# Conv-FFN of a hybrid transformer trunk: the tile epilogue in two parts, half a tile behind, and another order in the pool mixer

## The chip, the cores and the metric

The kernel runs on one core of one Trainium2 chip. Its metric is the device time of one execution in microseconds (us). TensorE (PE) does the matmuls, VectorE (DVE) and ScalarE (ACT) the work on their operands and results, SyncE (SP) starts the DMAs that bring weights, and GpSimd (POOL) does next to nothing. An engine works through its instructions in the order in which the program holds them; engines wait for each other by semaphores. Products collect in PSUM, in eight banks of 2 KB for each of 128 partitions.

## The reference

One step of a trunk of four layers on 384 tokens (128 of context, 256 latent) of width 1024, in f32. The token mixer of a layer is a gated MLP (layers 0 and 3), a pooling mixer (layer 1) or windowed attention (layer 2). A convolutional FFN follows in every layer:

```python
def conv_ffn(h, w_in, conv_w, conv_b, w_out):
    a, u = jnp.split(h @ w_in, 2, axis=-1)
    ap = jnp.pad(a, ((0, 0), (1, 1), (0, 0)))
    a = ap[:, :-2] * conv_w[0] + ap[:, 1:-1] * conv_w[1] + ap[:, 2:] * conv_w[2] + conv_b
    return (jax.nn.gelu(a) * u) @ w_out

# run_trunk, for every layer i
h = rms_norm(x, g_mix[i]) * (1 + sc1) + sh1
y = ...                                        # the mixer
x = x + gt1 * y
h = rms_norm(x, g_ffn[i]) * (1 + sc2) + sh2
x = x + gt2 * conv_ffn(h, w_ffn_in[i], ffn_conv_w[i], ffn_conv_b[i], w_ffn_out[i])
```

The shifts, scales and gates (sh, sc, gt) come from `silu(cond) @ w_ada + b_ada`, six vectors a layer ("adaLN" below). The inner width is 2816, so `w_in` gives 22 tiles of 128 columns of `a` and as many of `u`. The pooling mixer subtracts from each token the mean over a window around it (four window sizes, one for each group of 256 columns), and multiplies each group by a 256x256 matrix.

## The kernel before

**Weights.** All weights lie in one list of chunks of 128x1024 f32, in the order of use; SP streams them into five buffers (`wraw`). For more precise products each chunk is split in two: ACT copies it to the rounded `whi` (L353), DVE subtracts that from it to get `wlo` (L360). Activations are split in the same way: in `split_act` ACT makes `gh` or `hb` (L592), DVE `gl` or its twin (L593). `mm3` (L678) then issues three matmuls for each product: `whi` with the high part, `wlo` with the high part, `whi` with the low part. `w_get` takes the next chunk for PE and first issues the split (`w_split`) of the chunk that comes three later; a function given as `mid` is called between the `whi` and the `wlo` of that split. Four buffers hold split chunks.

**adaLN.** Chunks of `w_ada` are woven into the list between the weights of other layers' work. Each costs DVE two instructions (`junk`, L395), which `w_split` issues behind `wlo`. The table `EDGES` says how many weights of a phase pass before the first such chunk and how many follow the last; the phase "fi" is the FFN's first product.

**FFN (`ffn`).** The chunks "fr" compute tiles 0 and 1 together in four PSUM banks. Then tile f = 2 to 21 takes two chunks (kk = 0 and 1), each 24 matmuls, in a pair of banks: `pa` gets the convolution's input, `pu` the gate. Six banks rotate under the name `mm`; tile 3 has the two others (`psa` and `adaT`). Each tile has an epilogue in three steps:

- `epi_a`: only for the first NR[l] = 3, 4, 3, 3 tiles of layers 0 to 3, whose input is not yet normalised: DVE scales `pa` and `pu` into SBUF. These tiles leave their banks there.
- `epi_b`: ACT copies `pa` into the padded row `ab` (L722) and starts the convolution `ct` (L724); DVE adds the two other taps (L726, two instructions).
- `epi_c`: ACT's GELU of `ct` into `gg` (L735), DVE's product with the gate (L736), which reads `pu` from PSUM. Then `split_act`.

In tile f's loop pass, `epi_a` and `epi_b` of tile f - 1 come with chunk kk = 0, `epi_c` ahead of chunk kk = 1's split, and `split_act` behind it. Tile 3's epilogue waits until f = 5, where tiles 3 and 4 go together. `norm(3)` issues three steps of the normalised input with each chunk while f < NR[l].

**Pool (`pool`, layer 1).** For each of four groups: `first` multiplies the group's columns (L1022), `scaled` copies the product to SBUF with ACT, scaled by the norm (`u`, three buffers, and `us2`, whose last part DVE makes at L1036), `second` does the windows' means as matmuls (L1045 to L1049) and DVE adds them to `x` (L1052). After each 128 columns of `x`, `aft` makes operands of the FFN that follows. The order is written out at the end of the function.

The scheduler keeps each engine's instructions in the order in which the functions call them.

Of the kernel before, what the change touches and what calls it, by code (L numbers as in the profile page):

```python
# [62 lines left out]
}  # L63


EDGES = {(0, "gv"): (2, 1), (0, "go"): (5, 0), (3, "gv"): (5, 2), "fi": (8, 2), (3, "go"): (5, 2)}


AP_REST = {"qkv": 1}
# [215 lines left out]
class Prog:  # L285
# [395 lines left out]
    def ffn(self, l, pr, follow, stat_k):  # L681
# [6 lines left out]
        with self.tc.tile_pool(name=f"ffn{l}", bufs=1) as fp:  # L688
# [11 lines left out]
            def epi_a(f, pa, pu):  # L700
                if f >= NR[l]:
                    return f, pa, None, pu, None
                a1 = self.tmp.tile([128, T], F32, tag="sq", name="a1")
                nc.vector.tensor_tensor(out=a1, in0=pa[:, 0:T], in1=rbs, op=ALU.mult)
                be = self.tmp.tile([128, 4], F32, tag="be", name="be")
                nc.scalar.activation(be[:, 0:2], pa[:, T:TE], AF.Copy)
                nc.scalar.activation(be[:, 2:4], pu[:, T:TE], AF.Copy)
                u1 = fp.tile([128, T], F32, tag="u1", name="u1", bufs=2)
                nc.vector.tensor_tensor(out=u1, in0=pu[:, 0:T], in1=rbs, op=ALU.mult)
                return f, a1, be, u1, be[:, 2:4]  # L710

            def epi_b(st):
                f, a1, be, _, _ = st
                cw = [self.par[:, PCOLS["cw"][0] + (3 * l + i) * NF + f:][:, 0:1] for i in range(3)]
                cb = self.par[:, PCOLS["cb"][0] + l * NF + f:][:, 0:1]
                ab = abs_[f % 2]
                for c, (t0, t1) in enumerate(GRPS):
                    p0, p1 = pos[c]
                    if f < NR[l]:
                        nc.scalar.activation(ab[:, p0:p1], a1[:, t0:t1], AF.Identity, bias=be[:, c:c + 1])  # L720
                    else:
                        nc.scalar.activation(ab[:, p0:p1], a1[:, t0:t1], AF.Copy)  # L722
                t = self.tmp.tile([128, T + 1], F32, tag="ct", name="ct")
                nc.scalar.activation(t, ab[:, 1:T + 2], AF.Identity, scale=cw[1], bias=cb)  # L724
                for i in (0, 2):
                    nc.vector.scalar_tensor_tensor(out=t, in0=ab[:, i:i + T + 1], scalar=cw[i], in1=t,  # L726
                                                   op0=ALU.mult, op1=ALU.add)
                return t
# [30 lines left out]
            def norm(n):  # L759
                for _ in range(n):  # L760
                    next(steps, None)
# [14 lines left out]
                    if k > stat_k + 1:  # L776
                        norm(2)

            prev = [(0, b[0], b[1]), (1, b[2], b[3])]
            for f in range(2, NF):  # L780
                w0 = TE if f < NR[l] else T

                pa, pu = (p()[:, :w0] for p in ((self.ps_bank, self.px_bank) if f == 3 else (self.bank, self.bank)))
                now, prev = (prev, []) if f == 5 else (prev[:1], prev[1:])
                for kk in range(2):
                    if kk == 0:
                        sts = []
                        w = self.w_get("fi", mid=lambda: sts.extend([epi_a(*p) for p in now]))
                        ts = [epi_b(st) for st in sts]
                    else:  # L790
                        gs = [epi_c(st, t) for st, t in zip(sts, ts)]
                        w = self.w_get("fi")
                        for st, g in zip(sts, gs):
                            self.split_act(g, gh[st[0]], gl[st[0]])
                    if f < NR[l]:
                        norm(3)
                    for k4 in range(4):
                        k = 4 * kk + k4
                        r = (hh[:, k, :], hl[:, k, :]) if f < NR[l] else (nh[:, k, :], nl[:, k, :])
                        self.mm3([(pa, 256 * k4), (pu, 256 * k4 + 128)], w, r, k == 0, k == 7)  # L800
                prev.append((f, pa, pu))
            assert next(steps, 0) == 0 and len(prev) == 1
            sts = []
            self.w_split(self.n_get + 2, lambda: sts.extend([epi_a(*p) for p in prev]))
            g = epi_c(sts[0], epi_b(sts[0]))
            self.split_act(g, gh[NF - 1], gl[NF - 1])
            self.use(1 - self.cur)
            res, after = follow()
            self.out_proj("fo", gh, gl, NF, l, 5, after, mid=self.sqrt_table, after_chunk=1)
# [180 lines left out]
    def pool(self, l, j, prep, pr):  # L990

        nc = self.nc
        hh, hl = self.hh, self.hl
        with self.tc.tile_pool(name=f"pool{l}", bufs=1) as pp:
            mx = pp.tile([128, 4, 640], F32, tag="mx", name="mx")

            ms = pp.tile([66, 4, T], F32R, tag="ms", name="ms")
            us2 = pp.tile([66, 4, 256], F32R, tag="us2", name="us2")  # L1000
            nc.sync.dma_start(mx, self.a["mix"])
            nc.gpsimd.dma_start(ms, self.a["mixsum"])
            nc.gpsimd.memset(us2.bitcast(F32), 0.0)
            res, aft = prep()
            w = None
            us = {}

            def first(g):
                nonlocal w
                if g % 2 == 0:  # L1010
                    w = self.w_get("p")
                ps = [self.bank() for _ in range(2)]
                for i in range(4):
                    o = ps[i // 2][:, 256 * (i % 2):256 * (i % 2) + 256]
                    t = slice(128 * i, 128 * i + 128)
                    if i == 3:
                        o, t = o[0:2, :], slice(T, TE)
                    for p in range(3):
                        for kk in range(2):
                            k = 2 * g + kk  # L1020
                            c = 512 * (g % 2) + 256 * kk
                            nc.tensor.matmul(o, (hl if p == 2 else hh)[:, k, t], w[p == 1][:, c:c + 256],  # L1022
                                             start=(p == 0 and kk == 0), stop=(p == 2 and kk == 1),
                                             skip_group_check=True)
                us[g] = ps

            def scaled(g):
                ps = us[g]
                u = pp.tile([128, 3, 256], F32, tag="u", name="u", bufs=3)
                for i in range(3):  # L1030
                    nc.scalar.activation(u[:, i, :], ps[i // 2][:, 256 * (i % 2):256 * (i % 2) + 256], AF.Copy,
                                         scale=r[:, i:i + 1])
                sh = ps[1][0:2, 256:512]
                for q in (0, 64):
                    nc.scalar.activation(us2[q:q + 2, g, :], sh, AF.Copy)
                nc.vector.tensor_tensor(out=us2[32:34, g, :], in0=sh, in1=us2[0:2, g, :].bitcast(F32), op=ALU.subtract)  # L1036
                us[g] = u

            def second(g):
                u = us.pop(g)  # L1040
                for n in range(2):
                    d = 2 * g + n
                    ps = self.bank()[:, :T]
                    c = slice(128 * n, 128 * n + 128)
                    nc.tensor.matmul(ps, us2[:, g, c], ms[:, g, :], start=True, stop=False, skip_group_check=True)  # L1045
                    nc.tensor.matmul(ps[:, 0:TC], u[:, 0, c], mx[:, g, 0:128], start=False, stop=False,
                                     skip_group_check=True)
                    for i in range(2):
                        nc.tensor.matmul(ps[:, TC:T], u[:, 1 + i, c], mx[:, g, 128 + 256 * i:384 + 256 * i],  # L1049
                                         start=False, stop=(i == 1), skip_group_check=True)  # L1050
                    for cc, (t0, t1) in enumerate(GRPS):
                        nc.vector.scalar_tensor_tensor(out=self.x[:, d, t0:t1], in0=ps[:, t0:t1],  # L1052
                                                       scalar=self.pgs[:, d, cc:cc + 1], in1=self.x[:, d, t0:t1],
                                                       op0=ALU.mult, op1=ALU.add)
                    aft(d)

            first(0)
            r = self.stats(pr["acc"])
            first(1)
            scaled(0)  # L1060
            first(2)
            scaled(1)
            second(0)
            scaled(2)
            first(3)
            second(1)
            scaled(3)
            second(2)
            second(3)
            return res  # L1070
# [626 lines left out]
```

## Time and profile before

| | us |
|---|---|
| three runs, median (lowest to highest) | 1771.77 (1771.72 to 1775.01) |
| the profiled execution | 1772.34 |
| its span | 1770.6 |
| PE busy | 1748.9 |
| PE weight load busy | 1671.1 |
| DVE busy | 1347.4 |
| ACT busy | 885.5 |
| POOL busy | 3.4 |

The granted clock of PE was 0.999 of full speed over the span. Busy times come from one profiled execution; a merged row of the timeline covers successive instructions of one form, and matmuls overlap, so that a row's time is longer than the pitch between them. A wait is the idle time of an engine ahead of an instruction, put down to the instruction whose semaphore came last.

### The profile page before, as it was taken

The numbers are of one execution on the slowest core, as the hardware profiler recorded it, in microseconds if no ns is written. First come the engines' busy times: TensorE is split into PE (matmuls) and PEld (weight loads), VectorE is DVE, ScalarE is ACT, GpSimd is POOL, SyncE is SP. The second block draws the span as 40 slices with busy tenths as digits, with TensorE's granted clock in tenths as the row PEclk, the third lists the DMA queues.
The fourth block names the chain that finished last, engine by engine and source line by source line (L and its number), as shares of the span: only waits on it lengthen the run. The fifth ranks groups of instructions, "written<-read, shape, count | busy, mean of one in ns | idle before, by whom it ended". The sixth has DMA issues, their size and how long they took to land.

```text
span 1770.6 us, 26877 instructions
## 1 busy us (share of the span) xinstructions
PE 1748.9 (99%) x10282; PEld 1671.1 (94%) x10282; DVE 1347.4 (76%) x2309; ACT 885.5 (50%) x1661; POOL 3.4 (0%) x32
## 2 busy tenths in 40 slices
PE   9999999999999999999999999999999999999999
PEld 7799899999998999999778999999988999999999
DVE  6888778888986788886787788887775676876632
ACT  4644346444456654532568564553354444754521
POOL 0000000000000000000000000000000000000000
PEclk9999999999999999999999999999999999999999
DMA  9765654565662356566443336556645334354341
GB/s 338 281 220 167 230 196 139 195 199 188 232 219 106 108 190 202 185 226 208 175 150 132 119 132 200 191 173 202 196 166 192 119 132 155 118 180 147 133 155 54
DMA packets 87728, 312.03 MB, mean 176 GB/s; under 512 B 10478, under 2 KB 10990, under 8 KB 87344
## 3 DMA queue, kind: packets, MB, share of 16 engines
q1 hardware_dynamic: 87216, 309.91, 51.4%
q8 instruction: 80, 1.31, 0.3%
q0 software_dynamic: 96, 0.41, 0.1%
q14 instruction: 48, 0.39, 0.1%
q10 hardware_dynamic: 288, 0.01, 0.0%
HBM read 308.45 MB, written 1.84 MB: 175 GB/s over the span
## 4 chain that ended last, share of the span: by engine, by line
PE 79%; DVE 12%; ACT 5%; issue 3%; DMA 2%; ACTq 0%; DVEq 0%; SPq 0%
PE mm L678 60%; PE mm L852 6%; DVE wlo L360 4%; DVE junk L395 4%; ACT whi L353 2%; DMA wraw<-wts 2%; DVE ct L726 2%; PE adaT L678 2%; PE S L678 1%; PE psa L678 1%; PE mm L896 1%; PE S L1133 1%; PE adaT L852 1%; PE psa L852 1%; PE O L1353 0%
## 5 line engine op out<-in xcount | busy, mean ns | idle before, releaser
L678 PE MATMUL mm<-hb,whi 128*128 128x384 f32 (+1 forms) x3936 | 859.2, 337 | 0.0
L678 PEld LDWEIGHTS mm<-hb,whi 128*128 128x128 f32 x3936 | 698.2, 188 | 3.6 <-issue 1.2
L360 DVE TENSOR_TENSOR wlo<-wraw,whi 128x1024 fp32r<-128x1024 f32 (+2 forms) x390 | 466.0, 1201 | 211.7 <-ACT whi L353 211.2
L353 ACT ACTIVATE whi<-wraw 128x1024 fp32r<-128x1024 f32 (+2 forms) x390 | 399.6, 1034 | 252.2 <-PE mm L678 156.1
L678 PE MATMUL mm<-hb,wlo 128*128 128x384 f32 (+1 forms) x1968 | 504.5, 337 | 5.0 <-DVE wlo L360 4.9
L678 PEld LDWEIGHTS mm<-hb,wlo 128*128 128x128 f32 x1968 | 355.9, 188 | 7.8 <-DVE wlo L360 7.8
L395 DVE SCALAR_TENSOR_TENSOR junk<-wraw,condb 128x1024 bf16<-128x1024 f32 x288 | 351.9, 1222 | 7.9 <-ACT condb L1615 2.7
L735 ACT ACTIVATE gg<-ct 128x128 f32<-128x128 f32 (+1 forms) x150 | 46.4, 356 | 245.6 <-DVE ct L726 245.6
L678 PE MATMUL mm<-gh,wlo 128*128 128x384 f32 x448 | 123.3, 336 | 0.6 <-DVE wlo L360 0.6
L678 PE MATMUL mm<-gh,whi 128*128 128x384 f32 x448 | 123.3, 336 | 0.0
L678 PE MATMUL mm<-gl,whi 128*128 128x384 f32 x448 | 123.2, 336 | 0.0
L726 DVE SCALAR_TENSOR_TENSOR ct<-ab,par,ct 128x385 f32<-128x385 f32 x176 | 108.6, 619 | 6.2 <-ACT ct L724 2.5
L852 PE MATMUL mm<-whi,hb 128*128 128x512 f32 x320 | 87.2, 397 | 0.0
L613 ACT ACTIVATE hb<-x,A 128x128 fp32r<-128x128 f32 x96 | 42.5, 455 | 86.1 <-DVE x L468 80.4
L678 PEld LDWEIGHTS mm<-gh,wlo 128*128 128x128 f32 x448 | 81.7, 188 | 1.0 <-DVE wlo L360 1.0
L678 PEld LDWEIGHTS mm<-gh,whi 128*128 128x128 f32 x448 | 81.7, 188 | 0.1
L678 PEld LDWEIGHTS mm<-gl,whi 128*128 128x128 f32 x448 | 81.8, 188 | 0.0
L736 DVE TENSOR_TENSOR gg<-mm,gg 128x384 f32<-128x384 f32 x72 | 40.2, 558 | 47.2 <-ACT gg L735 46.5
L852 PEld LDWEIGHTS mm<-whi,hb 128*128 128x128 f32 x320 | 59.4, 187 | 17.2 <-issue 2.5
L724 ACT ACTIVATE ct<-ab,par 128x385 f32<-128x385 f32 x88 | 62.7, 713 | 3.4
L468 DVE SCALAR_TENSOR_TENSOR x<-mm,prm,x 128x128 f32<-128x128 f32 x92 | 33.6, 411 | 27.0 <-PE mm L678 27.0
L852 PE MATMUL mm<-wlo,hb 128*128 128x512 f32 x160 | 47.0, 399 | 0.0
(291 smaller groups left out, 1769.4 us busy)
## 6 DMA issues: line engine op xcount, KB each, us to landing
wraw<-wts SPq DMA_DIRECT2D x562, 512.0 KB, 3.9
wraw<-wts SPq DMA_DIRECT2D x12, 256.0 KB, 2.9
wraw<-wts SPq DMA_DIRECT2D x8, 384.0 KB, 4.3
x<-x SPq DMA_DIRECT2D x4, 384.0 KB, 4.5
mx<-mix SPq DMA_DIRECT2D x1, 1280.0 KB, 8.3
y<-x SPq DMA_DIRECT2D x3, 384.0 KB, 4.8
condb<-condb SPq DMA_DIRECT2D x1, 1024.0 KB, 6.5
ws<-a_w_s SPq DMA_DIRECT2D x2, 512.0 KB, 5.5
```

Of the source, the lines that this page charges most:

```text
L353: nc.scalar.activation(hi[:, :n], t[:, :n], AF.Copy)
L360: nc.vector.tensor_tensor(out=lo[:, :n], in0=t[:, :n], in1=hi[:, :n].bitcast(F32), op=ALU.subtract)
L395: nc.vector.scalar_tensor_tensor(out=self.junk.bitcast(BF16), in0=w, scalar=1.0, in1=self.condb[:, c, :], op0=ALU.mult, op1=ALU.mult, accu ...
L468: nc.vector.scalar_tensor_tensor(out=x[:, d, t0:t1], in0=ps[:, t0:t1], scalar=self.prm[:, l, ty * 8 + d, c:c + 1], in1=x[:, d, t0:t1], op0 ...
L613: nc.scalar.activation(self.hh[:, d, t0:t1], self.x[:, d, t0:t1], AF.Copy, scale=A[:, d, c:c + 1])
L678: nc.tensor.matmul(o, w[:, c:c + nw], r, start=(first and p == 0), stop=(last and p == 2))
L724: nc.scalar.activation(t, ab[:, 1:T + 2], AF.Identity, scale=cw[1], bias=cb)
L726: nc.vector.scalar_tensor_tensor(out=t, in0=ab[:, i:i + T + 1], scalar=cw[i], in1=t, op0=ALU.mult, op1=ALU.add)
L735: nc.scalar.activation(g[:, t0:t1], t[:, t0 + c:t1 + c], GELU)
L736: nc.vector.tensor_tensor(out=g, in0=u, in1=g, op=ALU.mult)
L852: nc.tensor.matmul(ps[n][i], hs, w[p == 1][:, c:c + 512], start=(k == 0 and p == 0), stop=(k == 7 and p == 2))
L896: nc.tensor.matmul(ps[:, 128 * i:128 * i + 128], v[:, i, 128 * c:128 * c + 128], ws[:, c // 2, :], start=True, stop=True)
```

## The change

One function, `epilogue(todo, get)`, now does the work around each chunk's split. It first takes the chunk (so `whi`, `epi_a` in the middle, `wlo` and adaLN's `junk`), then does `epi_c` and `split_act` of the tile that is due, then `epi_b` of the tile in `todo`, which is due at the next chunk. Tiles up to 3 enter at kk = 0, the others at kk = 1, where before all entered at kk = 0; so from tile 4 on `epi_b` comes one chunk later, and `epi_c` at kk = 0 of the tile after. Layer 1's first adaLN chunk in the FFN comes behind its 14th weight instead of its 11th, with as many in all, and while NR[l] > 3 each chunk takes two normings. In the pool `u` gets a fourth buffer, and `first(3)` comes ahead of `second(0)`.

```diff
@@ -63,7 +63,7 @@
 }
 
 
-EDGES = {(0, "gv"): (2, 1), (0, "go"): (5, 0), (3, "gv"): (5, 2), "fi": (8, 2), (3, "go"): (5, 2)}
+EDGES = {(0, "gv"): (2, 1), (0, "go"): (5, 0), (3, "gv"): (5, 2), (1, "fi"): (12, 2), "fi": (8, 2), (3, "go"): (5, 2)}
 
 
 AP_REST = {"qkv": 1}
@@ -776,34 +776,35 @@
                     if k > stat_k + 1:
                         norm(2)
 
-            prev = [(0, b[0], b[1]), (1, b[2], b[3])]
+
+            prev, due = [(0, b[0], b[1]), (1, b[2], b[3])], []
+
+            def epilogue(todo, get):
+
+                sts = []
+                w = get(lambda: sts.extend([epi_a(*p) for p in todo]))
+                for st, t in due:
+                    self.split_act(epi_c(st, t), gh[st[0]], gl[st[0]])
+                due[:] = [(st, epi_b(st)) for st in sts]
+                return w
+
             for f in range(2, NF):
                 w0 = TE if f < NR[l] else T
 
                 pa, pu = (p()[:, :w0] for p in ((self.ps_bank, self.px_bank) if f == 3 else (self.bank, self.bank)))
-                now, prev = (prev, []) if f == 5 else (prev[:1], prev[1:])
                 for kk in range(2):
-                    if kk == 0:
-                        sts = []
-                        w = self.w_get("fi", mid=lambda: sts.extend([epi_a(*p) for p in now]))
-                        ts = [epi_b(st) for st in sts]
-                    else:
-                        gs = [epi_c(st, t) for st, t in zip(sts, ts)]
-                        w = self.w_get("fi")
-                        for st, g in zip(sts, gs):
-                            self.split_act(g, gh[st[0]], gl[st[0]])
+                    todo = [prev.pop(0)] if f < 6 and kk == 0 or f > 4 and kk == 1 else []
+                    w = epilogue(todo, lambda mid: self.w_get("fi", mid=mid))
                     if f < NR[l]:
-                        norm(3)
+                        norm(2 if NR[l] > 3 else 3)
                     for k4 in range(4):
                         k = 4 * kk + k4
                         r = (hh[:, k, :], hl[:, k, :]) if f < NR[l] else (nh[:, k, :], nl[:, k, :])
                         self.mm3([(pa, 256 * k4), (pu, 256 * k4 + 128)], w, r, k == 0, k == 7)
                 prev.append((f, pa, pu))
             assert next(steps, 0) == 0 and len(prev) == 1
-            sts = []
-            self.w_split(self.n_get + 2, lambda: sts.extend([epi_a(*p) for p in prev]))
-            g = epi_c(sts[0], epi_b(sts[0]))
-            self.split_act(g, gh[NF - 1], gl[NF - 1])
+            epilogue(prev, lambda mid: self.w_split(self.n_get + 2, mid))
+            epilogue([], lambda mid: None)
             self.use(1 - self.cur)
             res, after = follow()
             self.out_proj("fo", gh, gl, NF, l, 5, after, mid=self.sqrt_table, after_chunk=1)
@@ -1026,7 +1027,7 @@
 
             def scaled(g):
                 ps = us[g]
-                u = pp.tile([128, 3, 256], F32, tag="u", name="u", bufs=3)
+                u = pp.tile([128, 3, 256], F32, tag="u", name="u", bufs=4)
                 for i in range(3):
                     nc.scalar.activation(u[:, i, :], ps[i // 2][:, 256 * (i % 2):256 * (i % 2) + 256], AF.Copy,
                                          scale=r[:, i:i + 1])
@@ -1060,11 +1061,11 @@
             scaled(0)
             first(2)
             scaled(1)
+            first(3)
+            scaled(2)
             second(0)
-            scaled(2)
-            first(3)
+            scaled(3)
             second(1)
-            scaled(3)
             second(2)
             second(3)
             return res
```

DVE in layer 0's FFN, from the first part of tiles 3 and 4 (two `ct` pairs on `ab_2351` and `ab_2350`) on, before. `adaT` is tile 3's `pu`; the `mm` under `gg` is that of tile 4, then 5:

```order
L726 SCALAR_TENSOR_TENSOR ct<-ab_2351,par,ct 128x385 x2
L726 SCALAR_TENSOR_TENSOR ct<-ab_2350,par,ct 128x385 x2
L736 TENSOR_TENSOR gg<-adaT,gg 128x384
L736 TENSOR_TENSOR gg<-mm,gg 128x384
L360 TENSOR_TENSOR wlo<-wraw,whi 128x1024
L593 TENSOR_TENSOR gl<-gg,gh 128x384 x2
L360 TENSOR_TENSOR wlo<-wraw,whi 128x1024
L395 SCALAR_TENSOR_TENSOR junk,prm<-wraw,condb 128x1024 x2
L726 SCALAR_TENSOR_TENSOR ct<-ab_2351,par,ct 128x385 x2
L736 TENSOR_TENSOR gg<-mm,gg 128x384
```

Both tiles' `ct` and both `gg` stood together, ahead of the next `wlo`. The same place now, from tile 3's `ct` on:

```order
L726 SCALAR_TENSOR_TENSOR ct<-ab_2351,par,ct 128x385 x2
L360 TENSOR_TENSOR wlo<-wraw,whi 128x1024
L736 TENSOR_TENSOR gg<-adaT,gg 128x384
L593 TENSOR_TENSOR gl<-gg,gh 128x384
L726 SCALAR_TENSOR_TENSOR ct<-ab_2350,par,ct 128x385 x2
L360 TENSOR_TENSOR wlo<-wraw,whi 128x1024
L395 SCALAR_TENSOR_TENSOR junk,prm<-wraw,condb 128x1024 x2
L736 TENSOR_TENSOR gg<-mm,gg 128x384
L593 TENSOR_TENSOR gl<-gg,gh 128x384
L360 TENSOR_TENSOR wlo<-wraw,whi 128x1024
```

Two `wlo`, a `junk` pair and tile 3's second part now stand between tile 3's `ct` and tile 4's `gg`; PE's second matmul of tile 7 waits for the latter in both programs.

PE in the pool, before, from the end of the third group's first product on (the `x2` rows with 2x256 are its shift):

```order
L1022 MATMUL mm<-whi,hb_84 2x256 x2
L1045 MATMUL mm<-ms,us_5001 128x384
L1046 MATMUL mm<-mx,u 128x128
L1049 MATMUL mm<-mx,u 128x256 x2
L1045 MATMUL mm<-ms,us_5001 128x384
L1046 MATMUL mm<-mx,u 128x128
L1049 MATMUL mm<-mx,u 128x256 x2
L1022 MATMUL mm<-whi,hb_84 128x256 x2
L1022 MATMUL mm<-wlo,hb_84 128x256 x2
```

The first group's means stood between the third and the fourth group. Now (each line number is one higher):

```order
L1023 MATMUL mm<-wlo,hb_84 128x256 x2
L1023 MATMUL mm<-whi,hb_84 128x256 x2
L1023 MATMUL mm<-whi,hb_84 2x256 x2
L1023 MATMUL mm<-wlo,hb_84 2x256 x2
L1023 MATMUL mm<-whi,hb_84 2x256 x2
L1046 MATMUL mm<-ms,us_5001 128x384
L1047 MATMUL mm<-mx,u 128x128
L1050 MATMUL mm<-mx,u 128x256 x2
```

The fourth group's rows come first, and the means follow without a break.

## Rows read from the trace of the kernel before

**Rows 1.** The page: span, busy times, and the matmuls of L678.
```profile
span 1770.6 us, 26877 instructions
...
PE 1748.9 (99%) x10282; PEld 1671.1 (94%) x10282; DVE 1347.4 (76%) x2309; ACT 885.5 (50%) x1661; POOL 3.4 (0%) x32
...
L678 PE MATMUL mm<-hb,whi 128*128 128x384 f32 (+1 forms) x3936 | 859.2, 337 | 0.0
```

**Rows 2.** PE's waits (total, times, longest): whole span, then 306:470, then 600:616.
```profile
PE mm L678 <- DVE wlo L360: 5.5, 8, 1.0
PE mm L1045 <- DVE us L1036: 3.5, 2, 3.4
...
PE mm L678 <- DVE wlo L360: 2.5, 4, 0.6
...
PE mm L678 <- DVE wlo L360: 1.5, 2, 0.8
```

**Rows 3.** Windows: layer 0 ahead of tile 4's epilogue; layer 3's tile loop.
```profile
core 0: us, PE busy (x) PEld busy (x) DVE busy (x) ACT busy (x) POOL busy (x), PEclk, DMA share, GB/s
281.50:302.60 21.10, 21.10 (x123) 21.07 (x122) 18.92 (x31) 10.67 (x21) 0.00 (x0) 1.00 0.55 176
...
1508.00:1675.00 167.00, 167.00 (x965) 167.00 (x964) 123.28 (x176) 95.34 (x184) 0.00 (x0) 1.00 0.44 151
```

**Rows 4.** Timeline of PE, layers 0, 1 (two places) and 2: start, duration, instruction, count.
```profile
306.28 1.06 PE L678 MATMUL mm<-hb,whi 128*128 128x384 f32 x4
...
596.04 0.62 PE L678 MATMUL mm<-hb,wlo 128*128 128x384 f32 x2 [0.98 <-DVE wlo L360]
...
618.29 1.01 PE L678 MATMUL mm<-hb,whi 128*128 128x384 f32 x4
...
1059.50 0.86 PE L678 MATMUL mm<-hb,whi 128*128 128x384 f32 x4
```

**Rows 5.** Timeline of DVE in layer 0's FFN, tiles 3 to 6.
```profile
302.60 2.46 DVE L726 SCALAR_TENSOR_TENSOR ct<-ab,par,ct 128x385 f32<-128x385 f32 x4
...
305.75 0.56 DVE L736 TENSOR_TENSOR gg<-mm,gg 128x384 f32<-128x384 f32 x1 [0.22 <-ACT gg L735]
306.70 1.22 DVE L360 TENSOR_TENSOR wlo<-wraw,whi 128x1024 fp32r<-128x1024 f32 x1 [0.39 <-ACT whi L353]
307.84 1.02 DVE L593 TENSOR_TENSOR gl<-gg,gh 128x384 fp32r<-128x384 f32 x2
...
309.91 1.22 DVE L395 SCALAR_TENSOR_TENSOR junk<-wraw,condb 128x1024 bf16<-128x1024 f32 x1
...
314.28 0.56 DVE L736 TENSOR_TENSOR gg<-mm,gg 128x384 f32<-128x384 f32 x1 [0.69 <-ACT gg L735]
...
322.35 0.56 DVE L736 TENSOR_TENSOR gg<-mm,gg 128x384 f32<-128x384 f32 x1 [0.69 <-ACT gg L735]
```

**Rows 6.** Timeline of ACT in layer 0's FFN, one tile's first part.
```profile
438.96 0.51 ACT L592 ACTIVATE hb<-gg 128x384 fp32r<-128x384 f32 x1
439.37 0.53 ACT L722 ACTIVATE ab<-mm 128x128 f32<-128x128 f32 x2
439.93 0.71 ACT L724 ACTIVATE ct<-ab,par 128x385 f32<-128x385 f32 x1
```

**Rows 7.** Timeline of DVE, tiles 3 and 4 in layers 1 and 2.
```profile
614.57 2.46 DVE L726 SCALAR_TENSOR_TENSOR ct<-ab,par,ct 128x385 f32<-128x385 f32 x4
...
1053.40 2.46 DVE L726 SCALAR_TENSOR_TENSOR ct<-ab,par,ct 128x385 f32<-128x385 f32 x4
```

**Rows 8.** Timeline of PE at the end of the pool.
```profile
550.92 0.42 PE L1045 MATMUL mm<-ms,us 66*128 66x384 f32 x1 [3.39 <-DVE us L1036]
...
554.50 1.53 PE L678 MATMUL mm<-hb,whi 128*128 128x386 f32 x4
```

**Rows 9.** Timeline of DVE at the end of the pool.
```profile
553.01 0.74 DVE L1052 SCALAR_TENSOR_TENSOR x<-mm,pgs,x 128x128 f32<-128x128 f32 x2
553.66 0.17 DVE L607 CAST hb<-prm 128x16 fp32r<-128x16 f32 x1
```

**Rows 10.** Window at the pool's end, columns as in rows 3.
```profile
552.00:555.00 3.00, 3.00 (x10) 2.53 (x10) 2.82 (x9) 1.82 (x5) 0.00 (x0) 0.52 0.00 0
```

## The prediction

> **What bounds the kernel now.** The head of the page comes first: TensorE (PE) is busy for 1748.9 of 1770.6 us and VectorE (DVE) for 76% [rows 1]. A gain can therefore come only from the 22 us in which PE stands still, or from PE work done at half clock; a loss can come from anything that makes PE stand still anew. The profiled execution took 1772.34 us, 1.74 more than its span and 0.57 more than the median of the three runs (1771.77). I sum against the profiled execution and take off 0.6 at the end.
>
> PE's list of waits is the second view, since it shows what the change could remove. In the FFN (L678) PE waited 8 times for `wlo`, DVE's half of a chunk's split, 5.5 us in all; in the pool mixer it waited 3.4 us once at L1045 [rows 2]. The same list by window places the FFN's eight: four behind 306 in layer 0, 2.5 us [rows 2]; the other four, 3.0 us, in layer 1: one of 0.98 at 596.04 [rows 4], two of together 1.5 up to 616 [rows 2], and about 0.6 behind. Layers 2 and 3 have none. Third, two windows of the tile loops: in layer 3's, PE is busy for all of 167 us, so one matmul takes 167.00 / 965 = 0.173 us, a chunk of 24 4.15 us and a tile (two chunks) 8.3; in layer 0, in the stretch ahead of the place that will matter, DVE works 18.92 of 21.10 us [rows 3]. It is nearly as full as PE, so its order matters.
>
> **Edit 1, splits ahead of GELU and gate: the waits removed.** After the change each chunk's `wlo` stands before the gate product `gg` and its split. In layer 0, `wlo` at 306.70 stood behind two `gg` and idled 0.39 us for ScalarE (ACT) [rows 5]; that order is gone. I count all of layer 0's 2.5 us. Each wait also shows its last matmul as a long one, 337 ns where the pitch is 173 [rows 1, 3], so 0.16 us more for each: 2.5 + 4 x 0.16 = 3.1 us. In layer 1 the first wait, 0.98 us at 596.04 [rows 4], belongs to a chunk whose `wlo` has the same work ahead of it as before and stays; the later first adaLN chunk (edit 3) comes behind it. Of the other three, 1.5 + 0.3 lie ahead of tile 7 and 0.6 + 0.16 behind it: 2.6 us.
>
> **Edit 2, half a tile behind: a wait added.** From tile 4 on, the epilogue's first part runs at the next tile's second chunk and its second part at the chunk after that. The second part holds the instruction that frees a PSUM bank: `gg` reads `pu` in place. Six banks rotate as pairs; tile 3 has its own pair, so tile 7 takes tile 4's pair, 8 takes 5's and so on. Tile 7's second matmul, the first into `pu`, therefore waits for `gg` of tile 4. Before, that was in time by little: `gg` ran from 305.75 to 306.31 [rows 5]; the four PE matmuls from 306.28 are the last two of tile 6 and the first two of tile 7 [rows 4], so tile 7's second started three pitches on, at 306.8.
>
> Now count what DVE has between the start of tile 3's `ct` (302.60, a place that both orders reach after the same work) and the end of tile 4's `gg`. Before: 306.31 - 302.60 = 3.7 us. After, in the changed order: `ct` of tile 3, 1.2 (half of 2.46 for four); a `wlo`, 1.14 (306.70 to 307.84) [rows 5]; `gg` of tile 3, 0.56; then tile 4's own first part, which ACT starts only after tile 3's `gh`: 0.41 (`gh`, start to start), 0.56 (`ab`), 0.71 (`ct`) [rows 6]; DVE's `ct`, 1.2; a `wlo`, 1.14; the `junk` pair of an adaLN chunk, 2.4 (309.91 and its twin); `gg` of tile 4, 0.56 [rows 5]. The sum is 9.9 us, so `gg` ends at 312.5, and PE waits 312.5 - 306.8 = 5.7 us, with 0.16 for the restart. All of layer 0's removed waits lie behind this point and are still gained: 5.7 + 0.2 - 3.1 = + 2.8, and one later tile with two adaLN chunks adds up to 0.4: + 3.0 us. From below: DVE idles 2.2 us in the 21 us before [rows 3], so even if all of that vanished 3.5 us of the wait stay.
>
> Layer 1: tile 3's `ct` starts at 614.57 [rows 7], with one `junk` pair (2.4) less ahead of it by edit 3: 612.15 + 9.9 = 622.1. The same four matmuls start at 618.29 [rows 4], so tile 7's second at 618.8, or 617.0 without the 1.8 us of waits removed ahead of it: the wait will read 5.1 us, but those 1.8 only make it longer; the end moves by 622.1 - 618.8 + 0.2 - 0.8 = + 2.7. Layer 2: 1053.40 + 9.9 = 1063.3 [rows 7]; the four matmuls at 1059.50 [rows 4], tile 7's second at 1060.0: 3.3 + 0.2 = + 3.5. Layer 3 has an adaLN chunk only every other tile, and DVE works 123 of 167 us [rows 3]: 0. FFN in all: 3.0 + 2.7 + 3.5 = **+ 9.2 us**.
>
> Only once a layer: afterwards DVE's cycle, 322.35 - 314.28 = 8.07 us with one adaLN chunk [rows 5], has the same instructions in the new order, with fewer handovers between engines, and is under PE's 8.3. Each later `gg` gains on PE. At the end of the loop the last tile's second part is about 1 us later on DVE, but PE is later by more: 0.
>
> "Perfetto Trace Analysis" of the Trainium skill, under "Matmuls", says that independent groups should rotate through PSUM banks so that evacuation overlaps the next group's matmuls; here they do rotate, and by that rule alone the shift of half a tile costs nothing and the sum is rival (c)'s, - 6.9. The rows above speak against it: three pairs leave the evacuation 3.7 us of DVE work, and the new order puts 9.9 there.
>
> **Edit 3, layer 1's first adaLN chunk later, and two instead of three normings a chunk:** the same instructions, moved; counted above as 2.4 us on DVE.
>
> **Edit 4, pool.** PE's fourth group moves ahead of the first group's means. The chain that ends the stage isn't PE's: DVE adds the means to `x` in eight steps, with the next sub-layer's operands between; the sixth begins at 553.01, and the CAST at 553.66 behind it gives `hb` to the FFN's first matmul [rows 9]. This chain holds the same work, so PE finishes its groups sooner and waits longer: some 5 us instead of 3.4 [rows 2, 8], until about 553.9 instead of 554.50. That is - 0.6, and - 1.2 if the half clock is over by then. ACT's scalings or DVE's `us` of group 3 could also hold the chain up; no row shows that order, so I take as much the other way: - 1.2 to + 1.2.
>
> **The clock.** After the idle 3.39 us before 550.92 [rows 8], the granted clock from 552 to 555 was 0.52, the 1.2 GHz level [rows 10]. That cost 3 x 0.48 = 1.4 us. Idle times of 5.7, 5.1 and 5 us are longer than that one, so I put 1.4 on layers 0 and 1, and + 1.4 - 1.2 = + 0.2 on the pool; 3.3 us in layer 2 is at the edge and I leave it out, with 1.4 kept for the range.
>
> **Sum:** 9.2 + 2.8 + 0.2 = + 12.2 us; 1772.34 + 12.2 = 1784.5, less 0.6 = **1784 us**.
>
> **Rivals.** (a) The same bank waits, without the clock falling: + 9.2 - 1.2 = + 8, so 1779.7. For it: of all the waits in rows 2 only one is long enough to judge by; against it: all the new ones are longer. (b) The bank waits are small. It needs DVE to reach `ct` of tile 3 some 3 us earlier in layers 0 to 2, of which the 2.2 us of idle could give most if the new order closed every gap. The waits become 2.7, 2.1 and 0.3, the ends move by 2.9 - 3.1, 0.5 - 0.8 and + 0.5, the pool by - 1.2, in sum - 1.2: about 1770.5, the same within 0.2%. (c) On the other side, faster: banks are free in time. That holds where `gg` of tile 4 ends by 306.8 in layer 0, so where DVE reaches tile 3's `ct` by 296.9; then only the removals count, 3.1 + 2.6 + 1.2 = 6.9 us: 1764.8. Against it stand 18.92 us of DVE work in 21.10 [rows 3]: there is no such slack. (d) The edit doesn't do what it says: `wlo` still late. Then 3.1 + 2.6 more: about 1790; the order shows `wlo` moved, so it gets little.
>
> **How the numbers follow.** Forecast 0.60 (1780.5 to 1790), (a) 0.20 (1776 to 1780.5), (b) 0.09, (c) 0.08, (d) and more waits than counted 0.03. The range leaves out (b), (c) and (d): 1775.8 to 1790. The bounds for same are 0.2% = 3.5 us, about what a measurement of this kernel can tell from no change: 1768.2 to 1775.3. Slower 0.83, same 0.09, faster 0.08.
>
> **What would show it.** Right: PE waits for DVE `gg` near tile 7 of layers 0, 1 and 2, of 5 to 6, 5 and 3 us, none in layer 3; the waits for `wlo` fall from 8 to one or two; rows with a clock of about 0.5 after them; PE's idle before FFN 1 grows to 5 us, with the `x` chain in its place. Wrong: no wait for `gg`; a full clock after 5 us idle; a wait for `gg` at every tile (then the steady cycle is longer than PE's, and far above 1790); or a `ct` of tile 3 that DVE reaches several us sooner.

## The result, and the profile after

The changed kernel takes 1787.95 us (median of four runs, 1787.04 to 1788.64) against 1773.39 us (1771.72 to 1775.35) for the kernel before: ratio 1.0081, 95% interval 1.0064 to 1.0099. It is 14.6 us slower. The profiled execution took 1787.66 us with a span of 1785.9, 15.3 more than the span before, at a granted clock of 0.992 where it was 0.999.

The head of the page after and its costliest group; the last column of a group is the idle time ahead of it and what ended most of it [rows 1]:

```profile
span 1785.9 us, 26869 instructions
...
PE 1754.4 (98%) x10282; PEld 1680.1 (94%) x10282; DVE 1350.3 (76%) x2309; ACT 897.2 (50%) x1661; POOL 3.4 (0%) x32
...
L678 PE MATMUL mm<-hb,whi 128*128 128x384 f32 (+1 forms) x3936 | 866.0, 339 | 18.7 <-DVE gg L736 14.1
```

DVE does the same work as before, 1350 us. PE stands still for about 10 us more, and is busy for 5.5 us more with the same matmuls, some of which now run at half clock (below).

PE's waits after, with total, number and longest [rows 2]:

```profile
PE mm L678 <- DVE gg L736: 14.1, 3, 5.6
PE mm L678 <- DVE hb L607: 4.6, 1, 4.6
...
PE mm L678 <- DVE wlo L360: 1.0, 1, 1.0
```

Of the eight waits for `wlo`, 5.5 us, one of 1.0 us is left. In their place stand three waits for `gg`, 14.1 us. The pool's wait of 3.4 us at its means has become one of 4.6 us at the FFN's first matmul. The three new waits stand at tile 7 of layers 0, 1 and 2 (timeline of PE; each row is the second matmul of the tile) [rows 4]:

```profile
312.04 0.69 PE L678 MATMUL mm<-hb,whi 128*128 128x384 f32 x1 [5.62 <-DVE gg L736]
...
627.19 0.69 PE L678 MATMUL mm<-hb,whi 128*128 128x384 f32 x1 [5.28 <-DVE gg L736]
...
1072.41 0.69 PE L678 MATMUL mm<-hb,whi 128*128 128x384 f32 x1 [3.21 <-DVE gg L736]
```

What DVE does meanwhile in layer 0, from tile 3's `ct` to tile 4's `gg` [rows 5]:

```profile
302.05 1.27 DVE L726 SCALAR_TENSOR_TENSOR ct<-ab,par,ct 128x385 f32<-128x385 f32 x2
303.24 1.22 DVE L360 TENSOR_TENSOR wlo<-wraw,whi 128x1024 fp32r<-128x1024 f32 x1
304.37 0.55 DVE L736 TENSOR_TENSOR gg<-adaT,gg 128x384 f32<-128x384 f32 x1
305.51 0.56 DVE L593 TENSOR_TENSOR gl<-gg,gh 128x384 fp32r<-128x384 f32 x1 [0.59 <-ACT gh L592]
306.70 1.28 DVE L726 SCALAR_TENSOR_TENSOR ct<-ab,par,ct 128x385 f32<-128x385 f32 x2 [0.63 <-ACT ct L724]
307.89 1.22 DVE L360 TENSOR_TENSOR wlo<-wraw,whi 128x1024 fp32r<-128x1024 f32 x1
309.03 1.22 DVE L395 SCALAR_TENSOR_TENSOR junk<-wraw,condb 128x1024 bf16<-128x1024 f32 x1
...
311.44 0.55 DVE L736 TENSOR_TENSOR gg<-mm,gg 128x384 f32<-128x384 f32 x1
```

From 302.05 to the end of `gg` at 311.99 that is 9.94 us, where 3.7 us stood before. DVE is idle for 1.2 us of it, both times for ACT (0.59 and 0.63 in the rows).

The clock behind each stand, that is a time in which PE does nothing (windows; third figure from the right is the granted clock) [rows 10]: layer 0, the FFN of layer 1 behind the pool, layer 1's tile 7, layer 2's:

```profile
311.00:317.00 6.00, 4.96 (x15) 4.96 (x16) 4.99 (x8) 3.56 (x6) 0.00 (x0) 0.50 0.56 193
...
557.60:563.00 5.40, 5.39 (x17) 5.40 (x18) 4.51 (x13) 3.18 (x9) 0.00 (x0) 0.50 0.00 0
...
627.20:631.00 3.80, 3.80 (x12) 3.80 (x13) 2.85 (x4) 3.53 (x6) 0.00 (x0) 0.50 0.41 140
...
1072.40:1078.50 6.10, 6.09 (x19) 6.09 (x20) 5.10 (x8) 3.56 (x6) 0.00 (x0) 0.50 0.50 176
```

Half of the time that PE works there is lost: with the tails about 2.6, 2.75, 2.1 and 3.0 us.

Where the 15.3 us arise is read from the start of the same chunk's first matmul in both traces, worked out by counting the matmuls (us; a lag is the start after less the start before, and what a stretch cost is the difference of two lags; the last column is e3, below):

```
place                                    before    lag after   lag fourth pair (below)
tile 7 of layer 0 starts                 306.72      -0.70       -0.70
its second chunk                         311.90      +6.68       -1.72
out-projection, chunk 4                  447.23      +4.47       +0.91
pool starts                              527.27      +3.47       +2.50
FFN 1's first matmul                     554.50      +3.11       +2.14
FFN 1, tile 2                            573.43      +4.98       +3.97
tile 7 of layer 1 starts                 618.68      +2.89       +1.87
its second chunk                         623.86      +9.33       +0.86
out-projection of layer 1, seventh chunk 767.71      +9.00       +4.67
tile 7 of layer 2 starts                1059.84      +8.92       +4.65
its second chunk                        1064.00     +15.31       +4.65
last chunk                              1763.54     +15.32       +4.66
```

### The profile page after: what moved, and what is told of

Same layout as the page of the kernel before. It is cut to its first block, busy times and chain, and to the rows that moved or that the text cites. A ratio compares the mean times of both kernels' runs of the same rounds, so it can differ in the third digit from the quotient of the medians.

```text
span 1785.9 us, 26869 instructions
## 1 busy us (share of the span) xinstructions
PE 1754.4 (98%) x10282; PEld 1680.1 (94%) x10282; DVE 1350.3 (76%) x2309; ACT 897.2 (50%) x1661; POOL 3.4 (0%) x32
## 4 chain that ended last, share of the span: by engine, by line
PE 89%; DVE 7%; ACT 3%; issue 1%; DVEq 0%; ACTq 0%
PE mm L678 70%; PE mm L853 6%; DVE wlo L360 2%; PE S L678 1%; PE adaT L678 1%; DVE junk L395 1%; PE mm L897 1%; PE psa L678 1%; PE S L1134 1%; PE adaT L853 1%; PE psa L853 1%; ACT whi L353 1%; PE psa L413 1%; PE spare L1530 1%; PE O L1354 0%
## 5 line engine op out<-in xcount | busy, mean ns | idle before, releaser
L678 PE MATMUL mm<-hb,whi 128*128 128x384 f32 (+1 forms) x3936 | 866.0, 339 | 18.7 <-DVE gg L736 14.1
L678 PEld LDWEIGHTS mm<-hb,whi 128*128 128x128 f32 x3936 | 704.2, 190 | 22.9 <-DVE gg L736 15.0
L678 PE MATMUL mm<-hb,wlo 128*128 128x384 f32 (+1 forms) x1968 | 506.8, 338 | 1.0 <-DVE wlo L360 1.0
L678 PEld LDWEIGHTS mm<-hb,wlo 128*128 128x128 f32 x1968 | 359.5, 190 | 1.3 <-DVE wlo L360 1.3
L678 PE MATMUL mm<-gl,whi 128*128 128x384 f32 x448 | 123.3, 336 | 0.0
L678 PE MATMUL mm<-gh,wlo 128*128 128x384 f32 x448 | 123.2, 336 | 0.0
L678 PE MATMUL mm<-gh,whi 128*128 128x384 f32 x448 | 123.1, 336 | 0.0
L592 ACT ACTIVATE gh<-gg 128x384 fp32r<-128x384 f32 x56 | 29.4, 526 | 113.8 <-DVE gg L736 91.2
L678 PEld LDWEIGHTS mm<-gl,whi 128*128 128x128 f32 x448 | 81.8, 188 | 0.0
L678 PEld LDWEIGHTS mm<-gh,whi 128*128 128x128 f32 x448 | 81.8, 188 | 0.0
L678 PEld LDWEIGHTS mm<-gh,wlo 128*128 128x128 f32 x448 | 81.7, 188 | 0.0
L592 ACT ACTIVATE hb<-gg 128x384 fp32r<-128x384 f32 x48 | 25.2, 526 | 88.4 <-DVE gg L736 59.4
L593 DVE TENSOR_TENSOR gl<-gg,gh 128x384 fp32r<-128x384 f32 x56 | 31.3, 559 | 33.1 <-ACT gh L592 33.1
```

What stands on the lines that cost most here:

```text
L592: nc.scalar.activation(hi, src, AF.Copy)
L593: nc.vector.tensor_tensor(out=lo, in0=src, in1=hi.bitcast(F32), op=ALU.subtract)
L678: nc.tensor.matmul(o, w[:, c:c + nw], r, start=(first and p == 0), stop=(last and p == 2))
```

## The experiments

Each difference is against runs of the kernel before beside it; their median moved between 1772.8 and 1774.1 us from one set to the next, so ratios with intervals are compared, not times.

**e1: the FFN's part alone.** Edit: the changed file with layer 1's entry of `EDGES`, the normings and the pool as before.

```diff
-EDGES = {..., (1, "fi"): (12, 2), "fi": (8, 2), (3, "go"): (5, 2)}
+EDGES = {..., "fi": (8, 2), (3, "go"): (5, 2)}
-                        norm(2 if NR[l] > 3 else 3)
+                        norm(3)
```

> The FFN's new epilogue alone (edits 1 and 2); layer 1's adaLN chunks, the normings and the pool as before. Theory (bank wait and clock): three PE waits for gg, 5.6 us in layer 0, 3.2 us in layer 2 as in the changed kernel, and in layer 1 about 5.3 + 2.4 = 7.7 us, since one adaLN pair more (2.4 us) lies ahead of tile 3's ct; each followed by half clock. The lags of the changed kernel over the FFNs were + 4.1, + 4.0 and + 6.4 us; with 2.4 more in layer 1 the sum is about + 17 us against before. Rival (pool or adaLN chunks are what costs): under + 5 us.

Measured: ratio 1.0072 (1.0055 to 1.0089), + 12.4 us between the medians, and + 15.0 us by span. The FFN's part holds nearly the whole loss. The 17 us are missed by size. By the lags, layer 1's FFN cost 6.3 us (2.29 to 8.63) and layer 2's 6.4, as expected; what the 17 had left out are 0.5 us that this trace was ahead at the start, and 1.2 us in the pool: PE stands there for 3.39 us as in the kernel before, but the granted clock behind it is 1.00 from 554.4 to 557, where the kernel before had 0.52. Layer 1's wait came in pieces, its own and ACT's `ab`:

```profile
PE mm L678 <- DVE gg L736: 3.2, 1, 3.2
PE mm L678 <- ACT ab L722: 2.3, 1, 2.3
PE mm L678 <- DVE wlo L360: 2.1, 3, 1.2
```

Without edit 3 DVE is later, and PE meets it at more places.

**e2: the pool alone.** Edit: `u` with four buffers, `first(3)` and `scaled(2)` ahead of `second(0)`, all else as before.

> The pool's order and fourth buffer alone. Theory: the x chain on DVE ends the stage as before, some 0.4 us sooner; PE idles 4.6 us in one piece ahead of the FFN instead of 3.4, and the half clock falls on the FFN's first chunk: + 1 to + 1.5 us against before. Rival A (PE bounds the pool, so that the order saves time): - 1 us or better. Rival B (the pool holds most of what the change lost): + 5 us or more.

Measured: ratio 1.0005 (0.9996 to 1.0014): no difference that can be told. Rival B falls, and rival A's - 1 us lies just outside the interval; the theory's + 1 to + 1.5 us lies inside it, and so does no change. The trace shows the wait of 4.6 us, and the lag grows from 0.2 at the pool's start to 1.8 us at FFN 1's tile 2: that is the half clock. Another 1.8 us of this execution arise near 845 us in layer 2's attention, where nothing was edited and the granted clock was 0.57 from 843 to 851.

**e3: a fourth pair of banks.** Edit, on the changed kernel:

```diff
-                pa, pu = (... for p in ((self.ps_bank, self.px_bank) if f == 3 else (self.bank, self.bank)))
+                pa, pu = (... for p in ((self.ps_bank, self.px_bank) if f % 4 == 3 else (self.bank, self.bank)))
```

> The changed kernel with a fourth pair of PSUM banks in the tile rotation: every fourth tile (3, 7, 11, ...) takes the pair that only tile 3 had, so tile f needs the banks of tile f - 4 and not f - 3; no engine's order is altered but for the banks' names. Theory: gg has 8.3 us more, the three waits of 5.6, 5.3 and 3.2 us vanish and the half clock behind them (2.6, 2.1, 3.0 us) too: 22 us less than the changed kernel, 6 us less than before (4.1 - 8.4 in layer 0, 4.0 - 7.5 in layer 1, 0 in layer 2, + 1.5 in the pool). Rival (the new order itself is slow, the banks only show it): PE waits for something else, and the time stays at + 8 or more against before.

Measured: ratio 1.0025 (1.0016 to 1.0035), + 4.6 us. The three waits for `gg` are gone and with them about 10 us, so the wait was for the bank. But the kernel isn't faster than before: neither the theory's - 6 nor the rival's + 8. PE has a new wait:

```profile
PE mm L678 <- ACT whi L353: 5.5, 2, 3.5
```

It stands at the FFN's end, at the out-projection's fourth chunk of layer 0 (ACT, then PE; the first row is tile 21's GELU):

```profile
445.38 0.61 ACT L735 ACTIVATE gg<-ct 128x128 f32<-128x128 f32 x2 [1.35 <-DVE ct L726]
446.62 0.52 ACT L592 ACTIVATE hb<-gg 128x384 fp32r<-128x384 f32 x1 [0.62 <-DVE gg L736]
447.05 1.99 ACT L353 ACTIVATE whi<-wraw 128x1024 fp32r<-128x1024 f32 x2
...
448.14 0.62 PE L678 MATMUL mm<-gh,whi 128*128 128x384 f32 x2 [3.53 <-ACT whi L353]
```

That `whi` stands behind the last tile's epilogue, which DVE reaches only then. In the kernel before, the two were nearly together (ACT, then PE):

```profile
446.09 1.99 ACT L353 ACTIVATE whi<-wraw 128x1024 fp32r<-128x1024 f32 x2
...
447.23 0.57 PE L678 MATMUL mm<-gh,whi 128*128 128x384 f32 x2
```

In e3 PE comes at 444.6 and stands. By the lags it is 2.8 us ahead just before this chunk and 0.9 us behind in it, and half clock follows (0.50 from 449.5 to 452.5). So in layer 0 the time that the removed waits for `wlo` gave back was asked for again at the FFN's end.

**e4: PE kept busy in the new waits.** Edit, on the changed kernel, ahead of tile 7's first matmul:

```diff
+                    if f == 7 and kk == 0 and l < 3:
+                        fb = self.ps_bank()[:, 0:T]
+                        for _ in range(12 if l == 2 else 24):
+                            nc.tensor.matmul(fb, w[0][:, 0:128], nh[:, 0, :], start=True, stop=True)
```

> The changed kernel with PE kept busy in the idle time: 24 more matmuls of 384 columns in layers 0 and 1, 12 in layer 2, ahead of tile 7, into a bank that nobody reads. The waits for gg end at the same time as in the changed kernel, since DVE sets them; only PE's idle ahead of them shrinks, from 5.6, 5.3 and 3.2 us by 4.2, 4.2 and 2.1. Theory (half clock follows the idle and costs 2.6 + 2.1 + 3.0 us by itself): about 7.5 us less than the changed kernel, + 7.5 against before. Rival (the clock's fall costs nothing by itself, PE would have waited anyway): no change against the changed kernel, + 15.

Measured: ratio 1.0047 (1.0032 to 1.0062), 6 us less than the changed kernel, with 60 matmuls more. The stretch at layer 0's tile 7, in which PE still waits:

```profile
312.00:314.00 2.00, 0.52 (x3) 0.20 (x2) 1.94 (x5) 0.00 (x0) 0.00 (x0) 1.00 0.74 262
314.00:316.00 2.00, 1.97 (x11) 1.98 (x12) 1.05 (x2) 1.96 (x5) 0.00 (x0) 1.00 0.71 227
```

The clock stays at 1.00. The half clock is a cost of its own, and it came from PE's standing still. By the lags the three layers are 1.5, 1.9 and 2.8 us shorter than in the changed kernel, 6.2 in all where the theory had about 7.5.

**e5: edit 1 alone.** Edit, on the kernel before:

```diff
-                        gs = [epi_c(st, t) for st, t in zip(sts, ts)]
                         w = self.w_get("fi")
+                        gs = [epi_c(st, t) for st, t in zip(sts, ts)]
```

> The kernel before with edit 1 alone: at kk = 1 the chunk is split first and GELU, gate and their split follow; nothing is half a tile behind, tiles 3 and 4 still go together at f = 5. Theory (bank wait comes from the shift, edit 2): gg of tile 4 has one wlo more ahead of it, so PE waits 0.5 us at tile 7 of layer 0 and nothing like 5 us; the waits for wlo in the tile loop go. What they are worth hangs on the FFN's end: if ACT's whi of the fourth out-projection chunk still starts near 446 us behind the last tile's epilogue, as in the run with the fourth pair, PE only gets there sooner and idles there: - 1 to - 3 us against before. By the prediction's own count (removed waits are all gained): - 5.7 + 0.5, about - 5. Rival (edit 1 lengthens DVE's chain by itself): + 3 or more.

Measured: ratio 1.0019 (1.0010 to 1.0029), + 3 us, the rival's time; the theory's and the prediction's own count are missed. Edit 1 makes waits for `gg` too, only smaller ones: 1.8 us at tile 8 of layer 0 and 2.8 us in layer 1. DVE ahead of the first of them, and PE:

```profile
314.09 1.22 DVE L360 TENSOR_TENSOR wlo<-wraw,whi 128x1024 fp32r<-128x1024 f32 x1
315.23 1.22 DVE L395 SCALAR_TENSOR_TENSOR junk<-wraw,condb 128x1024 bf16<-128x1024 f32 x1
...
317.64 0.55 DVE L736 TENSOR_TENSOR gg<-mm,gg 128x384 f32<-128x384 f32 x1
...
318.25 0.44 PE L678 MATMUL mm<-hb,whi 128*128 128x384 f32 x1 [1.78 <-DVE gg L736]
```

The `wlo` that moves ahead of `gg` takes its `junk` pair along, 3.6 us in all.

**e6: edit 3 alone.** Edit: layer 1's entry of `EDGES` and the normings, in the kernel before.

> The kernel before with edit 3 alone: layer 1's first adaLN chunk behind the 14th weight, two normings a chunk. Theory: two of layer 1's waits for wlo (1.5 us between 600 and 616) go or shrink, and DVE has the same work until the FFN's end, where its last epilogue still decides: 0 to - 1.5 us against before. Rival (it is a part of the loss): + 2 or more.

Measured: ratio 0.9988 (0.9978 to 0.9997), about 2 us faster; waits for `wlo` in all 4.1 us instead of 5.5. This part of the change is a gain, though a small one: the interval ends at 0.9997.

**e7: e3 with an earlier split at the FFN's end.**

```diff
-            epilogue(prev, lambda mid: self.w_split(self.n_get + 2, mid))
+            epilogue(prev, lambda mid: self.w_split(self.n_get + 4, mid))
```

> The run with the fourth pair once more, and at the FFN's end one chunk more is split ahead of the last two parts of the epilogue (so ACT's whi and DVE's wlo of the out-projection's fourth chunk stand before GELU of tiles 20 and 21). Theory (with the bank waits gone the shift is paid at the FFN's end, where whi stood behind the last epilogue): PE's idle of 3.5 us in layer 0 and 1.9 us in layer 1 for whi goes, with the half clock behind it: 6 to 8 us less than with the fourth pair alone, so - 2 to - 4 against before. Rival (DVE is too late for the whole stage): the idle moves to the next chunks, and the time stays within 2 us of the fourth pair's.

Measured: ratio 0.9991 (0.9981 to 1.0000), 6 us less than e3; both long waits for `whi` are gone. That settles what e3 had left open. The theory's - 2 is just missed. By the lags PE is 4.1 us ahead in the out-projection's fourth chunk of layer 0, 1.0 of it from before the FFN, and 0.4 us at the pool's start: three short waits for `wlo` (2.1 us) and the slowed matmuls beside them take the rest back. So layer 0 gains nothing even now. The stretch from FFN 1's tile 2 to the seventh chunk of layer 1's out-projection is 3.5 us shorter, of which edit 3 alone gave 2.2 in e6's trace.

**e8: e5 with the same earlier split.**

> Edit 1 alone (as e5_split_first) and the same earlier split at the FFN's end. Theory: the waits for wlo in the tile loop go and nothing takes their place at the end: - 4 to - 6 us against before, some 3 less than e5_split_first. Rival (the removed waits are worth nothing because DVE's whole work bounds the FFN): the same as e5_split_first.

Measured: ratio 1.0012 (1.0002 to 1.0022), not to be told from e5. The theory falls: PE is late there from its waits for `gg` and never gets to the chunk before its `whi`.

**e10: e7 with the pool of before.**

> The fourth pair, the earlier split at the FFN's end and the pool of before: the changed FFN without its bank wait and without the pool's order. Theory (the parts' costs add): the profile with the changed pool ended 3.0 us ahead of before and the pool alone cost 1.8 us in its profile, 0.7 us by time: - 4 to - 5 us by profile, - 2.5 to - 4 us by time against before. Rival (the pool's order only looks costly, since the half clock moves elsewhere): the same as with the changed pool, about - 1.7.

Measured: ratio 0.9984 (0.9975 to 0.9992), some 3 us faster than before, as expected by time; the interval overlaps with e7's.

**e11: edit 1 alone with the fourth pair, the earlier split and edit 3** (e8 with the edits of e3 and e6).

> Edit 1 alone (nothing half a tile behind) with the fourth pair, the earlier split at the FFN's end and layer 1's later adaLN chunks, pool as before. Theory (edit 1's own waits for gg, 2.0 and 2.8 us, are bank waits too): no wait for gg, the waits for wlo in the tile loops go, - 3 to - 6 us against before. Rival (they come from DVE's cycle, which edit 1 lengthens): waits of 2 us or more remain and it is slower than before.

Measured: ratio 0.9976 (0.9965 to 0.9987), some 4 us faster. No wait for `gg` is left; edit 3 does not touch layer 0, so e5's wait there was a bank wait. About 2 of the 4 us are edit 3's (e6). By the lags layer 0 is 1.5 us shorter than before; in e5 it was 0.2. That is what the fourth pair and the earlier split add to edit 1 there; whether these two would give as much without it was not tried.

**e12: less adaLN work ahead of tile 7.** Edit, on the changed kernel: `(0, "fi"): (16, 2)` in `EDGES`.

> The changed kernel with layer 0's first adaLN chunk in the FFN behind the 18th weight instead of the 10th: no junk pair is left between tile 3's ct and tile 4's gg (9.9 - 2.4 = 7.5 us) and three less stand ahead of it. Theory (the wait at tile 7 is DVE's chain against PE's clock time): gg of tile 4 ends before 306 us, no wait there and no half clock (8.4 us). The same 19 chunks now lie on fewer tiles, and a tile with two costs DVE some 10.4 us against PE's 8.3, so waits of 1 to 2 us come back later in layer 0; at the layer's end a gain of 2 to 8 us against the changed kernel is left. Rival (the wait is bound to the order itself, not to DVE's load): 5 us or more remain at tile 7.

Measured: ratio 1.0070 (1.0055 to 1.0086), no gain. Tile 7 has no wait for `gg` and full clock, as the theory has it: so the wait is a race of DVE's chain with PE, and no property of the order by itself. The rest was mis-sized: the waits came back at every second tile from 12 on, five of together 6.8 us at full clock. By the lags layer 0 costs 4.1 us as in the changed kernel (this trace was 1.0 us behind at its start, that one 0.6 ahead). The same DVE work on fewer tiles made PE wait as much in other places. Four of the five:

```profile
350.06 0.45 PE L678 MATMUL mm<-hb,whi 128*128 128x384 f32 x1 [0.45 <-DVE gg L736]
368.41 0.44 PE L678 MATMUL mm<-hb,whi 128*128 128x384 f32 x1 [1.44 <-DVE gg L736]
387.03 0.44 PE L678 MATMUL mm<-hb,whi 128*128 128x384 f32 x1 [1.70 <-DVE gg L736]
405.43 0.44 PE L678 MATMUL mm<-hb,whi 128*128 128x384 f32 x1 [1.49 <-DVE gg L736]
```

**e13: e11 with PE kept busy in the pool's idle time.** Edit, between `scaled(3)` and `second(2)`:

```diff
+            fb = self.ps_bank()[:, 0:T]
+            for _ in range(17):
+                nc.tensor.matmul(fb, us2[:, 0, 0:128], ms[:, 0, :], start=True, stop=True)
```

> The last kernel (edit 1 alone, fourth pair, earlier split at the FFN's end, layer 1's later adaLN chunks, pool of before) with 17 more matmuls of 384 columns in the pool's idle time of 3.39 us, behind the second group's means and ahead of the third's, into a bank that nobody reads. Theory (the half clock from 549 to 556 in that kernel follows this idle time): the clock stays at full speed, the FFN's first matmul comes where DVE's CAST lets it, about 0.5 us sooner, and its first chunk is 0.5 to 1 us shorter: 1 to 2 us less, so - 5 to - 7 against before. Rival (the clock falls for another reason, or the x chain on DVE hides it all): the same as that kernel, - 4.

Measured: ratio 0.9966 (0.9954 to 0.9979), - 5.6 us between the medians. The interval overlaps with e11's; by the lags the stretch from the pool's start to FFN 1's tile 2 is 1.2 us shorter than before, where e11's is 1.4 us longer. The windows at the pool's end, of e11 first, then of e13:

```profile
549.00:552.00 3.00, 2.57 (x8) 2.24 (x8) 2.74 (x8) 1.42 (x4) 0.00 (x0) 0.51 0.00 0
552.00:555.00 3.00, 3.00 (x10) 2.61 (x9) 2.75 (x9) 2.11 (x6) 0.22 (x6) 0.50 0.00 0
```

```profile
549.00:552.00 3.00, 2.18 (x13) 1.94 (x13) 2.33 (x6) 1.68 (x4) 0.00 (x0) 1.00 0.00 0
552.00:555.00 3.00, 2.81 (x16) 2.38 (x15) 2.94 (x10) 1.68 (x4) 0.26 (x6) 1.00 0.00 0
```

This kernel has the lowest ratio of all and is faster than both the kernel before and the changed one.

## Why the prediction was right, point by point

**The bank wait** was the right mechanism and the right size: 5.7, 5.1 and 3.3 us forecast, 5.62, 5.28 and 3.21 measured, none in layer 3. DVE's chain was put at 9.9 us; it took 9.94, 10.1 and 9.94. e3 shows that it is the bank, e12 that it is the time of DVE's chain. With the waits this long rival (b) falls, with the clock at 0.50 behind them rival (a), and with seven of eight waits for `wlo` gone rival (d).

**The removed waits**: from eight to one, as forecast. That layer 0's 3.1 us seem to come back as 3.2 (from + 6.68 to + 3.47) is partly luck: the first of the four waits lies in tile 7's first chunk and is gone already in the 6.68. The other three were worth 0.8 to 1.2 us each by the lags, 3.0 in all and not 2.3 as in the sum, since several matmuls beside each wait had been slow. What the removed waits are worth without the new ones was wrong, and with it rival (c)'s price of - 6.9 us. That rival was refuted by its condition, and would not have held either with the banks free in time: in e3 they are, and the time is + 4.6. In layer 0 of the changed kernel PE lost 7.4 us in tile 7's first chunk, and behind that delay the FFN's end passed without a wait. The prediction's sentence that the last tile's second part comes later on DVE "but PE is later by more: 0" named this cover; e3 took it away, and showed 3.5 and 1.9 us.

The Trainium skill's "Perfetto Trace Analysis", under "Matmuls", has independent groups rotate through PSUM banks so that evacuation overlaps the next group's matmuls. By that rule alone the shift would have cost nothing; this trace does not agree, with 14.1 us of waits. The same page of the Trainium skill, under "Matmul Optimizations", asks for all eight PSUM banks to be used; e3, whose tiles rotate through all eight, agrees, with none of these waits left.

**The clock** is the term that was mis-sized. It was put at 1.4 us a stand, from the one row with a clock of 0.52, nothing for layer 2, and + 0.2 for the pool with its other terms. Measured: 2.6, 2.1 and 3.0 us in layers 0 to 2, the most behind the shortest of the three waits, and 2.75 at the pool. The row of before [rows 10] was one case and taken for the size of all; it was also cut off early, since the granted clock from 555 to 557 was still 0.87, so that even that case cost 1.7 us. By layer, forecast and measured lag: layer 0 4.4 and 4.1; pool 0.2 and 1.5; layer 1 4.1 and 4.0; layer 2 3.5 and 6.4. Layer 2 and the pool make up the difference between 12.2 and 15.3 us of span; 0.6 us the other way lie ahead of the first changed instruction. The measured time lies 4 us above the forecast of 1784 us.

**The pool**: the `x` chain stayed, with its wait of 4.6 us (some 5 forecast), and FFN 1 started 0.4 us sooner relative to the pool's start (0.6 forecast). The half clock then fell on the FFN's first chunk wholly.

**Steady state**: no further wait for `gg` in the changed kernel, as forecast.

## What to carry to other kernels

Ask of a deferred epilogue which instruction in it frees a PSUM bank, and count what its engine has to do ahead of that against the time at which the matmul engine comes round to the bank. A short wait that one takes away on the critical engine is a gain only if the engine that caused it has no later date to keep: here the gain stood again as a wait of 3.5 us at the stage's end (e3), and when that date was moved (e7), short waits behind it still took layer 0's gain back. Cost a new stand of TensorE with the half clock behind it; where the stand could not be avoided, matmuls into an unused bank kept the clock up here (e4, e13).

## What the runs showed of the hardware

A single stand of PE of 1.78 us (e5, layer 0) was followed by the 1.2 GHz level, with 0.50 from 320 to 322 us, while the five of e12, up to 1.7 us, left the clock at 1.00. In layer 2's attention, which no edit touches, the clock fell in e6 behind two stands of 0.80 and 0.88 us (0.56 from 842 to 844), while in the kernel before, with 0.42 and 0.87 us at the same place, it stayed at 1.00. And the same stand of 2.79 us, at the same tile of layer 1, left the clock at 1.00 in e5 and brought it to 0.50 in e8 (the windows behind it, of e5, then of e8):

```profile
622.00:624.00 2.00, 2.00 (x12) 2.00 (x13) 1.61 (x3) 1.97 (x5) 0.00 (x0) 1.00 0.60 225
```

```profile
624.00:626.00 2.00, 2.00 (x8) 2.00 (x7) 1.61 (x3) 1.97 (x5) 0.00 (x0) 0.50 0.21 86
```

By the lags, tile 7's first chunk there cost 2.0 us in e5 and 4.8 us in e8. So one profiled execution of a kernel with such stands says little about whether the next one pays for them, and lags of single traces here carry 1 to 3 us of this; what decides between the two was not tried.
